# The up projection as seven half products, woven with the gate products of the next pair

## The chip, the cores and the metric

The kernel runs on one core of one Trainium2 chip. The metric is the device time of one execution in microseconds, as the median over runs; three runs of the kernel before gave 1347.74 us in the median (1342.84 to 1347.84). A change of less than 0.5 % (some 7 us) counts as no change here, since that is about what a measurement of this kernel can tell.

Names of engines as in the profile: PE is TensorE (matmul), PEld its weight load, DVE is VectorE, ACT ScalarE, POOL GpSimd, SP the engine that issues the loads.

## The reference, cut to what matters

The program is one inference step of a decoder layer: two token mixers (a Mamba-2 part and an RWKV-7 part), then a SwiGLU feed-forward network, a per-layer embedding gate and a final norm, for 512 prompt tokens and 64 sample tokens (576 columns) at model width 1024. Only the feed-forward network is touched:

```python
hf = rmsnorm(h, w['norm_ffn'])
h = h + (jax.nn.silu(hf @ w['w_gate']) * (hf @ w['w_up'])) @ w['w_down']
```

`w_gate` and `w_up` are 1024 x 2816 (D_FF = 22 tiles of 128 columns), `w_down` is 2816 x 1024, all float32.

## The kernel before, in words

Activations lie transposed: 128 channels on the partitions, 576 tokens in the free dimension, so `hf` is eight tiles of 128x576 (`XF`). Every float32 operand is split into a rounded high part and a low remainder (`split`, L186: ACT copies the high part, DVE or POOL subtracts it for the low part), and each product is three matmuls: high x high, high x low, low x high. A matmul takes 288 of the 576 columns (`HV`).

`linear` (L217) makes one inner tile of 128 channels: two weight blocks of 128x512 are loaded, split (`wsplit`, L196, into `whi`/`wlo`, two buffers each; DVE and POOL take turns with the low part) and used in 24 matmuls each, 48 in all.

The 22 inner tiles are worked off in eleven pairs. Pair 0 is plain: gate and up with `linear`, then `silu`, the product with the up tile, and `inner` (L1350), which splits the result into `ah`/`al` for the down projection; POOL subtracts `al`. From pair 1 on the two gate tiles of a pair are made by `gate_pair` (L1411) after the Strassen-Winograd scheme: the weights of the two tiles are four blocks (upper and lower half of the 1024 channels, first and second tile), the activations four blocks (upper and lower channels, first and second 288 tokens), and seven products of a block with a block, 12 matmuls each, stand for eight, 84 matmuls for 96. For it

- the sums of activation blocks `T1` to `T4` are formed and split once, behind pair 0 (the loop over `k` at L1377 to L1389: per `k` four subtractions on DVE, eight ACT copies and four low parts, two on DVE and two on POOL);
- for each pair the sums of weight blocks `sw` (s1 and s2 and s4 on DVE) and a21 in place (POOL, L1418) are formed;
- each of the seven weight operands is split by `product` (L1398) into `wh`/`wl`, three buffers each;
- five results are kept or joined: ACT copies them out of PSUM (`kept`, tile `e`), POOL adds them (L1429, L1434, L1435), DVE adds from PSUM and multiplies by the norm's `rstd`.

Behind each gate pair its two up tiles come from `linear`. After pair 5 `down(False)` multiplies inner tiles 0 to 11 with `w_down`, after pair 10 `down(True)` the other ten.

Nothing of the order on an engine is as written: the Tile framework schedules the recorded instructions of each engine by its own timeline and hands out the buffers of a tag by it, so an engine's queue is a fixed list, worked off in order, and each instruction waits for its inputs and for its buffer to come free. The weights come from one packed array `wts` in the order of use, by SP.

Of the kernel before, what the change touches and what calls it, by code (L numbers as in the profile page):

```python
# [75 lines left out]
def hybrid_step(ctx, tc, A):  # L76
# [107 lines left out]

    def split(src, pool, tags, shape, lo_eng=None, hi=None, lo=None, hi_eng=None, **kw):
        hi = hi if hi is not None else pool.tile(shape, F32R, tag=tags[0], name=nm(tags[0]), **kw)  # L186
        lo = lo if lo is not None else pool.tile(shape, F32R, tag=tags[1], name=nm(tags[1]), **kw)
# [6 lines left out]
        eng.tensor_tensor(lo[:], src, hi[:].bitcast(F32), ALU.subtract)  # L194
# [1175 lines left out]


# [34 lines left out]
    def kept(ps):  # L1406
        t = cm.tile([P, HALF], F32, tag="e", name=nm("e"), bufs=5)
# [3 lines left out]
    def gate_pair():  # L1411

        a11, a21, a22 = (block() for _ in range(3))
        a12 = block(wp, "raw")
        s1, s2, s4 = (cm.tile([P, 512], F32, tag="sw", name=nm("sw"), bufs=3) for _ in range(3))
# [4 lines left out]
        ab, cc = lin_bank(), lin_bank()  # L1420
        a, b, c = ab[:, 0:HALF], ab[:, 512:512 + HALF], cc[:, 0:HALF]
        sa, sb = ft("sa"), ft("sb")
        product(a, a11, "B11", True, V)
        p1 = kept(a)
        product(b, s2, "T2", True, G)
        p6 = kept(b)
        product(c, s1, "T1", True, V)
        p5 = kept(c)
        G.tensor_tensor(p6[:], p6[:], p1[:], ALU.add)  # L1429
        product(a, a12, "B21", False, G)  # L1430
        V.tensor_tensor(sa[:, N1], a, rs[:, N1], ALU.mult)
        product(b, a21, "T3", False, V)
        p67 = kept(b)
        G.tensor_tensor(p67[:], p67[:], p1[:], ALU.add)  # L1434
        G.tensor_tensor(sb[:, N2], p67[:], p5[:], ALU.add)  # L1435
        product(c, s4, "B22", False, G)
        V.tensor_tensor(sa[:, N2], c, p6[:], ALU.add)
        V.tensor_tensor(sa[:, N2], sa[:, N2], rs[:, N2], ALU.mult)
        product(b, a22, "T4", False, V)
        V.tensor_tensor(sb[:, N1], b, p1[:], ALU.add)  # L1440
        V.tensor_tensor(sb[:], sb[:], rs[:], ALU.mult)
        for s_ in (sa, sb):
            act(s_[:], s_[:], AF.Silu)
        return sa, sb
# [12 lines left out]
    for p in range(1, NFF // 2):  # L1457
        for s_ in gate_pair():
            up = lin_ps()
            linear(XF, up, WLAST)  # L1460
            V.tensor_tensor(s_[:], up, s_[:], ALU.mult)
# [73 lines left out]
def pack(inp):  # L1535
# [79 lines left out]
    for c in range(0, NFF, 2):  # L1615
        if c:
            for ks, i in ((lo4, 0), (lo4, 1), (hi4, 1), (hi4, 0)):
                put(wg, ks, c + i)
        for i in range(2):
            if not c:  # L1620
                put_tile(wg, 0, 8, i)
            put_tile(wu, 0, 8, c + i)
# [50 lines left out]
```

## Time and profile before

| | us |
|---|---|
| median of three runs | 1347.74 |
| span of the profiled execution | 1349.0 |
| PE busy in it | 1246.8 |
| DVE / ACT / POOL busy in it | 826.0 / 618.9 / 625.6 |
| gate and up of pairs 1 to 5 (first product at 885.8, last before the down projection at 1017.5) | 131.7 |
| gate and up of pairs 6 to 10 (1097.0 to 1213.9) | 116.9 |

The span runs from the first to the last instruction; the page names no other time for this execution, and the median run is 1.3 us shorter than its span. The feed-forward network lies between some 875 us and 1287 us. A line of the profile's groups gives source line, engine, operation, output<-inputs, shape and count, then the summed and the mean duration, then the idle time of the engine before these instructions and what ended it.

### The profile page before, as it was taken

What the parts mean: (1) busy time and instruction counts of PE and PEld (TensorE: products, weight loads), DVE (VectorE), ACT (ScalarE), POOL (GpSimd) and SP (SyncE); (2) the same over time, 40 slices, a digit from 0 to 9 for tenths busy, and PEclk for the clock granted to TensorE, in tenths of its full rate; (3) what the DMA queues carried; (4) which work ended last, traced back from release to release, by engine and by line L of the source; (5) the groups of instructions that cost most, each with busy time, mean ns of one, the idle gap of its engine ahead of it and who ended that gap; (6) DMA issues with size and microseconds to landing.
All of it is one profiled execution on the core that took longest, in us unless ns stands there. A gap on an engine that the chain in (4) does not pass through costs nothing.

```text
span 1349.0 us, 26596 instructions
## 1 busy us (share of the span) xinstructions
PE 1246.8 (92%) x10525; PEld 1150.7 (85%) x10525; DVE 826.0 (61%) x1443; ACT 618.9 (46%) x1256; POOL 625.6 (46%) x597
## 2 busy tenths in 40 slices
PE   6897999999989978899999969989999999999997
PEld 6787897889868957788779859889999999999997
DVE  6648666887687785943466667886553135443454
ACT  6565436534654463343434364464442124433363
POOL 5425413642355154122456645565654336654642
PEclk9897799899979978889989989998999999999998
DMA  5322242234232412262454542222323222314322
GB/s 164 125 68 66 77 117 63 85 103 116 75 99 78 109 41 80 94 214 83 157 176 131 179 125 72 73 93 88 92 88 87 79 86 82 93 59 149 96 89 71
DMA packets 94461, 135.58 MB, mean 100 GB/s; under 512 B 34705, under 2 KB 39057, under 8 KB 94337
## 3 DMA queue, kind: packets, MB, share of 16 engines
q1 hardware_dynamic: 93760, 133.36, 32.4%
q8 instruction: 83, 1.36, 0.4%
q10 hardware_dynamic: 576, 0.52, 0.1%
q14 instruction: 42, 0.34, 0.1%
HBM read 106.10 MB, written 27.75 MB: 99 GB/s over the span
## 4 chain that ended last, share of the span: by engine, by line
PE 63%; DVE 14%; ACT 4%; issue 4%; DMA 3%; POOL 3%; DVEq 0%; SPq 0%; ACTq 0%; POOLq 0%
PE lin L234 21%; PE lin L1403 8%; PE lin L223 6%; PE lin L221 6%; PE lin L222 6%; DVE h L395 2%; PE lin L1508 1%; PE lin L1509 1%; PE lin L1510 1%; DVE tmp L674 1%; DVE wlo L206 1%; DVE Tt L676 1%; PE lin L613 1%; PE cx L797 1%; DVE suv L831 1%
## 5 line engine op out<-in xcount | busy, mean ns | idle before, releaser
L206 POOL TENSOR_TENSOR wlo<-raw,whi 128x512 fp32r<-128x512 f32 (+1 forms) x108 | 146.4, 1356 | 352.5 <-ACT whi L93 269.5
L93 ACT ACTIVATE whi<-raw 128x512 fp32r<-128x512 f32 (+1 forms) x232 | 143.3, 618 | 259.1 <-PE lin L234 126.4
L221 PE MATMUL lin<-xhi,whi 128*128 128x288 f32 (+1 forms) x784 | 243.3, 311 | 2.5 <-ACT whi L93 2.2
L223 PE MATMUL lin<-xhi,wlo 128*128 128x288 f32 (+1 forms) x784 | 241.5, 308 | 2.3 <-POOL wlo L206 2.3
L222 PE MATMUL lin<-xlo,whi 128*128 128x288 f32 (+1 forms) x784 | 241.5, 308 | 0.3 <-POOL xlo L194 0.3
L206 DVE TENSOR_TENSOR wlo<-raw,whi 128x512 fp32r<-128x512 f32 (+1 forms) x124 | 100.9, 814 | 103.2 <-PE lin L234 60.4
L221 PEld LDWEIGHTS lin<-xhi,whi 128*128 128x128 f32 (+1 forms) x784 | 151.0, 193 | 9.3 <-ACT whi L93 2.6
L223 PEld LDWEIGHTS lin<-xhi,wlo 128*128 128x128 f32 (+1 forms) x784 | 150.7, 192 | 6.2 <-POOL wlo L206 2.8
L222 PEld LDWEIGHTS lin<-xlo,whi 128*128 128x128 f32 (+1 forms) x784 | 150.8, 192 | 4.8 <-issue 1.2
L234 PE MATMUL lin<-xhi,whi 128*128 128x288 f32 x384 | 62.3, 297 | 3.2 <-ACT xhi L93 3.0
L234 PE MATMUL lin<-xlo,whi 128*128 128x288 f32 x384 | 60.8, 298 | 0.0
L234 PE MATMUL lin<-xhi,wlo 128*128 128x288 f32 x384 | 59.3, 297 | 0.0
L234 PEld LDWEIGHTS lin<-xhi,whi 128*128 128x128 f32 x384 | 54.6, 189 | 3.8 <-ACT xhi L93 1.7
L234 PEld LDWEIGHTS lin<-xlo,whi 128*128 128x128 f32 x384 | 54.8, 191 | 0.0
L234 PE MATMUL lin<-ah,wlo 128*128 128x288 f32 x352 | 54.7, 296 | 0.0
L234 PE MATMUL lin<-al,whi 128*128 128x288 f32 x352 | 54.7, 296 | 0.0
L234 PE MATMUL lin<-ah,whi 128*128 128x288 f32 x352 | 54.7, 296 | 0.0
L234 PEld LDWEIGHTS lin<-xhi,wlo 128*128 128x128 f32 x384 | 54.3, 191 | 0.0
L1403 PE MATMUL lin<-T,wh 128*128 128x288 f32 x320 | 50.1, 296 | 4.5 <-DVE T L194 2.8
L674 DVE TENSOR_TENSOR tmp<-L,Tt 72x30 f32<-72x30 f32 (+14 forms) x120 | 49.2, 410 | 3.2
L234 PEld LDWEIGHTS lin<-ah,whi 128*128 128x128 f32 x352 | 49.6, 189 | 0.0
L234 PEld LDWEIGHTS lin<-ah,wlo 128*128 128x128 f32 x352 | 49.6, 189 | 0.0
(425 smaller groups left out, 3197.8 us busy)
## 6 DMA issues: line engine op xcount, KB each, us to landing
raw<-wts SPq DMA_DIRECT2D x271, 256.0 KB, 2.6
S<-s_wkv SPq DMA_DIRECT2D x8, 512.0 KB, 5.1
hd<-s_ssm SPq DMA_DIRECT2D x8, 512.0 KB, 4.5
o_ssm_s<-hd SPq DMA_DIRECT2D x8, 512.0 KB, 2.9
xbc_d<-E SPq DMA_DIRECT2D x12, 288.0 KB, 2.1
x<-xT SPq DMA_DIRECT2D x8, 288.0 KB
gate_d<-g SPq DMA_DIRECT2D x8, 288.0 KB, 2.5
bv_d<-rw SPq DMA_DIRECT2D x8, 288.0 KB
```

What stands on the lines that cost most here:

```text
L93: return S.activation(out, in_, func, bias=bias, scale=scale)
L206: eng.tensor_tensor(lo[:, 0:n], raw[:, 0:n], hi[:, 0:n].bitcast(F32), ALU.subtract)
L221: T.matmul(ps[:, a:b], whi, xhi[:, a:b], start=first, stop=False)
L222: T.matmul(ps[:, a:b], whi, xlo[:, a:b], start=False, stop=False)
L223: T.matmul(ps[:, a:b], wlo, xhi[:, a:b], start=False, stop=last)
L234: T.matmul(ps[:, a:e], (hi, lo)[p][:, i * P:(i + 1) * P], xs[k + i][q][:, a:e], start=n == k + i == 0, stop=n == 2 and k + i == nk - 1, sk ...
L395: V.scalar_tensor_tensor(h[:], E[:, i:i + 600], w(i), h[:], ALU.mult, ALU.add)
L613: T.matmul(ps[:, c:c + 128].rearrange("p (a t) -> p a t", a=2), s.BK[jj][H[e], g].rearrange("p a t -> p (a t)"), s.G[H[e], g, jj, :, e], s ...
L674: V.tensor_tensor(o, L[:, jx:jx + 1, jx + 1:32].to_broadcast([NB, jx, n]), Tt[:, 0:jx, jx:jx + 1].to_broadcast([NB, jx, n]), ALU.mult)
L676: V.tensor_tensor(Tt[:, 0:jx, jx + 1:32], Tt[:, 0:jx, jx + 1:32], o, ALU.subtract)
L797: T.matmul(uw[H[e], jj, :], TT[H[e], g, jj, :], xs[H[e], jj, :], start=True, stop=True)
L1403: T.matmul(ps, (hi, lo)[p][:, k * P:(k + 1) * P], OPS[n][k][q], start=first and p == q == k == 0, stop=p == 1 and k == 3, skip_group_check ...
```

## The change

Five things, in the words of the diff:

1. The up tiles of a pair are made by seven half products too. `gate_pair` becomes `seven(up, out, order)`, a generator that yields after every product; `weave` runs two of them in turn, the gate of the next pair beside the up of this one. A pair then has 14 products of 12 matmuls in place of 7 and of four times 24.
2. Two pairs are plain instead of one (`for f in range(3)` ahead of the `T` sums and `for f in range(3, 4)` behind them), so nine pairs are left: four in the first weave, five in the second.
3. Joins read PSUM: DVE adds from PSUM to an `e` tile; ACT keeps only the first product, and POOL adds nothing any more. POOL instead forms a21 and s4 of each `seven` and the low part of two of its seven weight operands ("4" and "2"); DVE makes the other five. A fourth PSUM place `d` holds product 4.
4. `inner` no longer has POOL subtract `al` for the first eight of the inner tiles of each down projection: ACT writes minus the source, rounded like the high part, and a DMA issued by POOL adds the source to it (`accum_op`). Tiles 8 and up keep the subtraction.
5. Buffers: seven weight blocks, four `sw`, eight `e`; the reserve for POOL's DMA descriptors is set to 1024 bytes of each partition (no DMA was issued by POOL before). The packed weights are put in the new order.

```diff
+    def below(lo, src, hi, eng):
+        if eng == "D":
+            act(lo, src, scale=-1.0)
+            G.dma_start(lo, src, accum_op=ALU.add)
+        else:
+            eng.tensor_tensor(lo, src, hi.bitcast(F32), ALU.subtract)
...
-        AF2.append(split(s_[:], fp, (f"ah{f}", f"al{f}"), [P, NT], lo_eng=G))
+        AF2.append(split(s_[:], fp, (f"ah{f}", f"al{f}"), [P, NT], lo_eng="D" if f % 12 < 8 else G))
 
-    for f in range(2):
+    for f in range(3):
         ps = lin_ps()
         linear(XF, ps, WLAST)
...
+    for f in range(3, 4):
+        ps = lin_ps()
+        linear(XF, ps, WLAST)
...
-        t = pool.tile([P, 512], F32, tag=tag, name=nm(tag), bufs=3)
+        t = pool.tile([P, 512], F32, tag=tag, name=nm(tag), bufs=7)
...
-    def gate_pair():
-        a11, a21, a22 = (block() for _ in range(3))
-        a12 = block(wp, "raw")
-        s1, s2, s4 = (cm.tile([P, 512], F32, tag="sw", name=nm("sw"), bufs=3) for _ in range(3))
+    def seven(up, out, order):
+        a11, a22, a21, a12 = (block() for _ in range(4))
+        s1, s2, s4 = (cm.tile([P, 512], F32, tag="sw", name=nm("sw"), bufs=4) for _ in range(3))
         V.tensor_tensor(s1[:], a21[:], a22[:], ALU.add)
         V.tensor_tensor(s2[:], s1[:], a11[:], ALU.subtract)
         G.tensor_tensor(a21[:], a11[:], a21[:], ALU.subtract)
-        V.tensor_tensor(s4[:], a12[:], s2[:], ALU.subtract)
...
+        G.tensor_tensor(s4[:], a12[:], s2[:], ALU.subtract)
...
+        def join(dst, ps, x):
+            if up:
+                t = kt()
+                V.tensor_tensor(t[:], ps, x[:], ALU.add)
+                V.tensor_tensor(dst, dst, t[:], ALU.mult)
+            else:
+                V.tensor_tensor(dst, ps, x[:], ALU.add)
+        for step in order:
+            if step == "1":
+                product(a, a11, "B11", True, V)
+                e[1] = kept(a)
+            elif step == "6":
+                product(b, s2, "T2", True, V)
+                e[2] = kt()
+                V.tensor_tensor(e[2][:], b, e[1][:], ALU.add)
+            elif step == "4":
+                product(d, a22, "T4", True, G)
+            elif step == "7":
+                product(b, a21, "T3", False, V)
+                e[3] = kt()
+                V.tensor_tensor(e[3][:], b, e[1][:], ALU.add)
+                join(sb[:, N1], d, e[3])
+            elif step == "5":
+                product(c, s1, "T1", True, V)
+                join(sb[:, N2], c, e[3])
+                if not up:
+                    V.tensor_tensor(sb[:], sb[:], rs[:], ALU.mult)
+                    act(sb[:], sb[:], AF.Silu)
+            elif step == "2":
+                product(a, a12, "B21", False, G)
+                V.tensor_tensor(sa[:, N1], a, (sa if up else rs)[:, N1], ALU.mult)
+            else:
+                product(c, s4, "B22", False, V)
+                join(sa[:, N2], c, e[2])
+                if not up:
+                    V.tensor_tensor(sa[:, N2], sa[:, N2], rs[:, N2], ALU.mult)
+                    act(sa[:], sa[:], AF.Silu)
+            yield
+    def weave(pairs, first):
+        queue = [(up, out) for out in ([] for _ in range(pairs)) for up in (False, True)]
+        live, n = [], 0
+        while live or queue:
+            if queue and (not live or len(live) == 1 and n >= (1 if first else 4)):
+                up, out = queue.pop(0)
+                live.append((seven(up, out, "1647523" if first else "1647523"), up, out))
+                n = 0
+                first = first and not up
+            for t in list(live):
+                if next(t[0], 1):
+                    live.remove(t)
+                    if t[1]:
+                        for s_ in t[2]:
+                            inner(s_)
+            n += 1
...
-    for p in range(1, NFF // 2):
-        for s_ in gate_pair():
-            up = lin_ps()
-            linear(XF, up, WLAST)
-            V.tensor_tensor(s_[:], up, s_[:], ALU.mult)
-            inner(s_)
-        if p == NSPLIT - 1:
-            down(False)
+    weave(NSPLIT - 2, True)
+    down(False)
+    weave(NFF // 2 - NSPLIT, False)
...
-    nc = _bacc.Bacc("TRN2", target_bir_lowering=False, num_devices=1)
+    nc = _bacc.Bacc("TRN2", target_bir_lowering=False, num_devices=1, dynamic_dma_scratch_size=1024)
```

Ahead of the feed-forward network no engine's queue differs. Inside it three places carry the prediction.

DVE in the middle of the first weave before (a row is source line, operation, output<-inputs, shape; L1416, L1417, L1419 are s1, s2, s4 of the next gate, L194 and L206 low parts of weights, L1440 and L1461 reads of PSUM, L1441 a product in SBUF):

```order
L1416 TENSOR_TENSOR sw_10994<-raw_1733_10988,raw_1734_10990 128x512
L1461 TENSOR_TENSOR sa_10722<-lin_10854,sa_10722 128x576
L1417 TENSOR_TENSOR sw_10995<-sw_10994,raw_1732_10986 128x512
L1419 TENSOR_TENSOR sw_10996<-raw_10992,sw_10995 128x512
L1440 TENSOR_TENSOR sb_10723<-lin_10720,e_10740 128x288
L194 TENSOR_TENSOR wl_11042<-sw_10994,wh_11041 128x512
L1441 TENSOR_TENSOR sb_10723<-sb_10723,rstd_9895 128x576
L206 TENSOR_TENSOR wlo_11169<-raw_11166,whi_11168 128x512
```

DVE in the change, in the second half of a pair of the first weave (L1436 and L1437 are s1 and s2 of the gate after the next, L191 low parts, L1454, L1479 and L1463 reads of PSUM, L1475 a product in SBUF; `sb` and `sa` are the gate tiles, `lin_11131` belongs to the up):

```order
L1436 TENSOR_TENSOR sw_11269<-raw_1801_11265,raw_1800_11263 128x512
L1454 TENSOR_TENSOR sb_10979<-lin_10977,e_11094 128x288
L191 TENSOR_TENSOR wl_11187<-sw_10971,wh_11186 128x512
L1479 TENSOR_TENSOR sa_10978<-lin_10976,rstd_9895 128x288
L1475 TENSOR_TENSOR sb_10979<-sb_10979,rstd_9895 128x576
L1437 TENSOR_TENSOR sw_11270<-sw_11269,raw_1799_11261 128x512
L1463 TENSOR_TENSOR e_11184<-lin_11131,e_11149 128x288
L191 TENSOR_TENSOR wl_11222<-raw_1773_11120,wh_11221 128x512
L1454 TENSOR_TENSOR sa_10978<-lin_10977,e_11031 128x288
L191 TENSOR_TENSOR wl_11243<-sw_11124,wh_11242 128x512
L191 TENSOR_TENSOR wl_11281<-raw_1799_11261,wh_11280 128x512
```

The same stretch holds more low parts and more short joins, and s4 has left the queue.

POOL beside it, in the change (L1439 is s4, L1438 a21, L191 low parts, L189 the issue of an adding transfer):

```order
L1439 TENSOR_TENSOR sw_11126<-raw_1774_11122,sw_11125 128x512
L191 TENSOR_TENSOR wl_11152<-raw_1741_10967,wh_11151 128x512
L189 DMA al_1763_11069<-sa_10724 128x576
L1438 TENSOR_TENSOR raw_1801_11265<-raw_1799_11261,raw_1801_11265 128x512
L191 TENSOR_TENSOR wl_11206<-raw_1772_11118,wh_11205 128x512
L1439 TENSOR_TENSOR sw_11271<-raw_1802_11267,sw_11270 128x512
L191 TENSOR_TENSOR wl_11299<-raw_1774_11122,wh_11298 128x512
```

POOL's queue now alternates between a sum that needs DVE's s1 or s2 and the low part that PE needs, with the transfers between; the adds of `e` tiles are gone.

PE before, while the `T` sums are being made (L1403 is a product, L234 a plain matmul of `linear`; a row with x2 is both halves of the columns):

```order
L1403 MATMUL lin_10159<-T_1571_10067,wh_10198 128x288
L234 MATMUL lin_10292<-xhi_9634,whi_10325 128x288 x2
L234 MATMUL lin_10292<-xhi_9675,whi_10325 128x288 x2
L234 MATMUL lin_10292<-xhi_9716,whi_10325 128x288 x2
L234 MATMUL lin_10292<-xhi_9757,whi_10325 128x288 x2
L234 MATMUL lin_10292<-xlo_9635,whi_10325 128x288 x2
L234 MATMUL lin_10292<-xlo_9676,whi_10325 128x288 x2
L1403 MATMUL lin_10158<-T_1573_10069,wh_10180 128x288
```

PE in the change at the end of the second plain pair (L241 a plain matmul, L1424 a product; `lin_10422` is the first gate, `lin_10477` its up):

```order
L241 MATMUL lin_10340<-xhi_9634,wlo_10374 128x288 x2
L241 MATMUL lin_10340<-xhi_9675,wlo_10374 128x288 x2
L241 MATMUL lin_10340<-xhi_9716,wlo_10374 128x288 x2
L241 MATMUL lin_10340<-xhi_9757,wlo_10374 128x288 x2
L1424 MATMUL lin_10422<-xlo_9553,wh_10426 128x288
L1424 MATMUL lin_10422<-xlo_9594,wh_10426 128x288
L1424 MATMUL lin_10422<-xhi_9471,wl_10427 128x288
L1424 MATMUL lin_10422<-xhi_9511,wl_10427 128x288
```

Before, products with `T` stand between the plain matmuls as soon as one part of `T` is expected; in the change all 96 plain matmuls of inner tile 3 and the first product of the gate stand ahead of any matmul with `T`, and the up's first product follows.

More of the change, by code (lines that the diff above doesn't have):

```diff
@@ L192, in split @@
         flip[0] += 1
-        eng = lo_eng or (G if flip[0] % 2 else V)
-        eng.tensor_tensor(lo[:], src, hi[:].bitcast(F32), ALU.subtract)
+        below(lo[:], src, hi[:], lo_eng or (G if flip[0] % 2 else V))
         return hi, lo
@@ L1390, in hybrid_step @@
         OPS[n] = [tuple(XF[k0 + k][i][:, c] for i in range(2)) for k in range(4)]
+    for f in range(3, 4):
+        ps = lin_ps()
+        linear(XF, ps, WLAST)
+        if f == 0:
+            up = lin_ps()
+            linear(XF, up, WLAST)
+            rs = rstd_of(st)
+        s_ = ft("sg")
+        V.tensor_tensor(s_[:], ps, rs[:], ALU.mult)
+        act(s_[:], s_[:], AF.Silu)
+        if f:
+            up = lin_ps()
+            linear(XF, up, WLAST)
+        V.tensor_tensor(s_[:], up, s_[:], ALU.mult)
+        inner(s_)
     def block(pool=cm, tag="raw2"):
-        t = pool.tile([P, 512], F32, tag=tag, name=nm(tag), bufs=3)
+        t = pool.tile([P, 512], F32, tag=tag, name=nm(tag), bufs=7)
         nc.sync.dma_start(t[:], A["wts"][wat[0]:wat[0] + P * 512].rearrange("(p n) -> p n", p=P))
@@ L1406, in kept @@
     def kept(ps):
[L1407 removed]
+        t = cm.tile([P, HALF], F32, tag="e", name=nm("e"), bufs=8)
         act(t[:], ps)
         return t
[L1411 to L1415 removed]
+    def seven(up, out, order):
+        a11, a22, a21, a12 = (block() for _ in range(4))
+        s1, s2, s4 = (cm.tile([P, 512], F32, tag="sw", name=nm("sw"), bufs=4) for _ in range(3))
         V.tensor_tensor(s1[:], a21[:], a22[:], ALU.add)
@@ L1418, in gate_pair @@
         G.tensor_tensor(a21[:], a11[:], a21[:], ALU.subtract)
-        V.tensor_tensor(s4[:], a12[:], s2[:], ALU.subtract)
[L1420 to L1444, printed above, removed]
+        G.tensor_tensor(s4[:], a12[:], s2[:], ALU.subtract)
+        ab, cd = lin_bank(), lin_bank()
+        a, b, c, d = (t[:, i:i + HALF] for t in (ab, cd) for i in (0, 512))
+        kt = lambda: cm.tile([P, HALF], F32, tag="e", name=nm("e"), bufs=8)
+        if not up:
+            out += [ft("sa"), ft("sb")]
+        sa, sb = out
+        e = [None] * 4
@@ new lines, in join @@
+        def join(dst, ps, x):
[32 more added lines that the diff above has]
+                join(sa[:, N2], c, e[2])
+                if not up:
+                    V.tensor_tensor(sa[:, N2], sa[:, N2], rs[:, N2], ALU.mult)
+                    act(sa[:], sa[:], AF.Silu)
+            yield
@@ L1616, in pack @@
         if c:
[L1617 to L1622, printed above, removed]
+            for w in (wg, wu) if c >= 4 else ():
+                for ks, i in ((lo4, 0), (hi4, 1), (lo4, 1), (hi4, 0)):
+                    put(w, ks, c + i)
+        for i in range(4) if not c else ():
+            put_tile(wg, 0, 8, i)
+            put_tile(wu, 0, 8, i)
         if c // 2 in (NSPLIT - 1, NFF // 2 - 1):
```

1 line of the change is left out of this document (added).

## The prediction

> **What bounds the kernel now.** I read the page's busy times first, then the busy times by stretch, then what PE waits for, then the single instructions of one pair.
>
> ```profile
> span 1349.0 us, 26596 instructions
> PE 1246.8 (92%) x10525; PEld 1150.7 (85%) x10525; DVE 826.0 (61%) x1443; ACT 618.9 (46%) x1256; POOL 625.6 (46%) x597
> ...
> core 0: us, PE busy (x) PEld busy (x) DVE busy (x) ACT busy (x) POOL busy (x), PEclk, DMA share, GB/s
> 860.00:870.00 10.00, 7.60 (x59) 7.14 (x58) 9.57 (x7) 3.97 (x7) 7.69 (x5) 1.00 0.17 54
> 900.00:910.00 10.00, 6.74 (x47) 5.98 (x45) 9.79 (x14) 6.37 (x14) 7.46 (x8) 1.00 0.08 26
> 910.00:920.00 10.00, 8.75 (x45) 8.76 (x46) 3.41 (x6) 2.72 (x5) 2.90 (x3) 0.66 0.29 82
> 920.00:930.00 10.00, 9.76 (x74) 9.56 (x73) 8.38 (x11) 4.35 (x9) 6.24 (x5) 1.00 0.24 78
> 955.30:979.30 24.00, 24.00 (x184) 24.00 (x183) 12.69 (x16) 11.14 (x21) 14.06 (x11) 1.00 0.32 95
> ```
>
> In a settled pair (955.3 to 979.3) PE is busy without a gap and the other engines about half the time. PE alone bounds it. The exception is the start, 900 to 930, where DVE is full and PE is not. What PE waits for from 876 to 1290 is all there:
>
> ```profile
> PE lin L1403 <- DVE T L194: 2.8, 1, 2.8
> PE lin L1403 <- ACT T L93: 1.7, 2, 1.0
> ...
> 963.27 1.60 PE lin L1403 x12
> 964.87 3.18 PE lin L234 x24
> ```
>
> The last two rows are from the chain of waits and give the price of a matmul: 3.18 us / 24 = 0.1325 us.
>
> **What the change removes on PE.** Four plain tiles more, two less: before, 2 plain tiles x 2 x 48 + 10 x (84 + 96) = 1992 matmuls; after, 4 x 2 x 48 + 9 x 168 = 1896. Minus 96 matmuls x 0.1325 = **-12.7 us**. All of it lies on the path as long as PE stays full. A pair falls from 180 x 0.1325 = 23.9 to 168 x 0.1325 = 22.3 us.
>
> **The start.** From 900 to 930 PE did 47 + 45 + 74 = 166 matmuls where 3 x 75.5 = 226 fit. The 60 missing cost 60 x 0.1325 = 8.0 us: the waits for `T` (4.5 us), then a stretch at a granted clock of 0.66. Forming `T` keeps DVE from
>
> ```profile
> 889.12 1.69 DVE L1382 TENSOR_TENSOR tt<-xa 128x288 f32<-128x288 f32 x1
> ...
> 911.12 0.44 DVE L194 TENSOR_TENSOR T<-xb,T 128x288 fp32r<-128x288 f32 x1
> ```
>
> that is 22.4 us. In the change PE meanwhile has the up of tile 2 (48), tile 3 (96) and the first products of gate and up (24): 168 x 0.1325 = 22.3 us. The work just covers; I keep 1.5 us for the first matmuls with `T`, and take **-6.5 us** (bounds -4 to -8).
>
> **What the change adds on the other engines.** The rows of 926 to 1020 (pairs 2 to 5 of the kernel before), by form:
>
> ```profile
> L194 DVE TENSOR_TENSOR wl<-raw,wh 128x512 fp32r<-128x512 f32 x12 | 10.9, 912 | 5.5 <-ACT wh L93 5.5
> L1417 DVE TENSOR_TENSOR sw<-sw,raw 128x512 f32<-128x512 f32 x4 | 5.3, 1335 | 0.0
> L1416 DVE TENSOR_TENSOR sw<-raw,raw 128x512 f32<-128x512 f32 x4 | 3.1, 784 | 2.2 <-DMA raw<-wts 2.1
> L1441 DVE TENSOR_TENSOR sb<-sb,rstd 128x576 f32<-128x576 f32 x5 | 7.0, 1406 | 2.1 <-POOL sb L1435 2.1
> L1431 DVE TENSOR_TENSOR sa<-lin,rstd 128x288 f32<-128x288 f32 x4 | 1.8, 458 | 17.1 <-PE lin L1403 17.1
> L1438 DVE TENSOR_TENSOR sa<-sa,rstd 128x288 f32<-128x288 f32 x4 | 1.8, 451 | 0.0
> ...
> L1418 POOL TENSOR_TENSOR raw<-raw,raw 128x512 f32<-128x512 f32 x5 | 7.0, 1396 | 13.7 <-DVE sw L1416 13.7
> L194 POOL TENSOR_TENSOR al<-sa,ah 128x576 fp32r<-128x576 f32 x5 | 9.0, 1805 | 0.0
> L194 POOL TENSOR_TENSOR wl<-raw,wh 128x512 fp32r<-128x512 f32 x4 | 5.6, 1408 | 2.2 <-ACT wh L93 2.2
> ...
> L93 ACT ACTIVATE wh<-raw 128x512 fp32r<-128x512 f32 x16 | 10.0, 625 | 10.0 <-PE lin L1403 4.7 <-POOL wlo L206 3.1 <-issue 2.2
> L93 ACT ACTIVATE e<-lin 128x288 f32<-128x288 f32 x15 | 5.6, 401 | 3.9 <-PE lin L1403 3.9
> L93 ACT ACTIVATE ah<-sa 128x576 fp32r<-128x576 f32 x5 | 3.4, 683 | 0.9 <-DVE sa L1461 0.8
> ```
>
> A pair then asks of DVE 10 low parts x 0.91, two s1 x 0.78, two s2 x 1.34, twelve joins from PSUM x 0.46, four short SBUF products x 0.45 and one `sb` x `rstd` of 1.41: 9.1 + 1.6 + 2.7 + 5.5 + 1.8 + 1.4 = 22.1 us, against 12.7 before. Of ACT 14 x 0.63 + 2 x 0.40 + 6 x 0.68 = 13.7 us, in most pairs with two more copies for `al`: 15.1. Of POOL 4 x 1.41 + 4 x 1.40 = 11.2 us and two transfers to issue. ACT and POOL fit into 22.3; **DVE is as long as PE.** What a pair costs is decided there.
>
> ```profile
> 882.29 0.69 DVE L206 TENSOR_TENSOR wlo<-raw,whi 128x512 fp32r<-128x512 f32 x1 [1.93 <-PE lin L234]
> 882.90 0.69 DVE L1416 TENSOR_TENSOR sw<-raw,raw 128x512 f32<-128x512 f32 x1
> 883.50 0.75 DVE L1363 TENSOR_TENSOR sg<-lin,rstd 128x576 f32<-128x576 f32 x1
> ...
> 991.48 1.88 POOL L194 TENSOR_TENSOR al<-sa,ah 128x576 fp32r<-128x576 f32 x1
> 993.32 1.25 POOL L1435 TENSOR_TENSOR sb<-e,e 128x288 f32<-128x288 f32 x1
> ...
> 992.07 1.83 DVE L206 TENSOR_TENSOR wlo<-raw,whi 128x512 fp32r<-128x512 f32 x1
> 993.83 0.44 DVE L1440 TENSOR_TENSOR sb<-lin,e 128x288 f32<-128x288 f32 x1
> ```
>
> The DVE means hold a stall. With POOL idle a 128x512 subtract starts 0.61 us after the last one; with POOL on `al` the same subtract took 1.83 us and ended 0.54 us after POOL's end (993.36). A read of PSUM took 0.44 us though POOL ran. So the two engines take turns when both operands lie in SBUF: a meeting costs DVE what is left of POOL's instruction.
>
> [...]
>
> I walk the second half of a pair with that (the DVE and POOL rows shown with the change). From the end of product 5 PE has 4 + 12 + 8 + 12 + 4 matmuls before product 7, and 8 more before it needs that low part: 48 x 0.1325 = 6.4 us. DVE and POOL take turns meanwhile: s1 0.6, a21 1.4, low part 0.6, POOL's low part 1.4, `sb` x `rstd` 0.7, s2 0.6, s4 1.4, low part of product 7 0.6: 7.3 us, the reads of PSUM hidden beside POOL. PE waits 0.9 us there. The next low part but one (product 1 of the next gate) meets POOL's low part of product 2, for 0 or 1.2 us, as it falls. The first half has room: seen the same way its low parts end 0.6 us or more before their use. So PE waits 0.9 to 2.1 us a pair; the last pair of each weave has no s1 and s2 of a following one, and so less. I take **1.0 us for each of nine pairs, +9 us**.
>
> Bounds of this term: 0 (the queues meet less often than walked), and 2.7 a pair: 2.1 and another 0.6 where the issue of a transfer holds POOL longer than the 1.0 us that I allow. The trace has no DMA issued by POOL; the nearest row is the subtract it replaces, 1.8 us, which is nearly the upper end, and nothing is the lower. The landing of the transfer has no reader before the down projection. ACT's second copy (0.68) stands ahead of the high part of the second product behind it, with 1.6 us of room.
>
> **Sum.** 1349.0 - 12.7 - 6.5 + 9.0 = 1338.8 us of span. The median of the runs lies 1.3 us below that span: **1338 us** (1337.5), 0.7 % faster.
>
> **Rivals.**
>
> *All waits are hidden* (0 to 0.4 a pair): 1347.7 - 19.2 + 2 = 1330 us. For it: PE had no wait in any settled pair; against it: DVE was then half idle. 0.13.
>
> *The gain is given back* (1.4 to 2.8 us a pair, about 2.1): 1347.7 - 19.2 + 19 = 1347 us. This is the change not doing what it says: PE has less to do and waits as much longer. For it: the second meeting of the walk, lost each time. 0.25.
>
> *The shared turn becomes the bound*, and the kernel slower. Per pair the SBUF instructions of both engines, one after the other, are 14 x 0.61 + 0.7 + 4 x 0.4 + 8 x 1.4 = 22.0 us; the reads of PSUM (twelve, at 0.4 us from start to start) add 4.8 where they don't fall beside POOL. If none does, a pair takes 26.8 us, PE waits 4.5, and the time is 1347.7 - 19.2 + 40 = 1369 us; with half of them, 24.4 and 1347. It is slower than before by over 0.5 % from 2.9 us a pair, when under a third falls beside POOL. In pairs whose `al` stays on POOL (three of nine) 2 x 1.5 us are added. For it: DVE's sum of 22.1; against it: 993.83, where a read did fall beside POOL. I give 0.16, and say 1358.
>
> *The clock falls.* After the waits for `T` the granted clock was 0.66 from 910 to 920 (45 matmuls in 8.75 us), though in 860 to 870, with PE busy 7.60 of 10, it stayed at 1.00. Some 3 us were lost by it. If it came in every pair: 1338 + 27 = 1365 us. The waits of my walk are about 1 us among 22 of work, less than in 860 to 870. 0.03.
>
> [...]
>
> **How the numbers follow.** My forecast (0.4 to 1.4 us a pair, 1332 to 1341 us) has 0.43, and with the hidden case 0.56 lies below 1341, faster by over 0.5 % (about what a measurement can tell from no change). The range runs from 1327 (-8.0 at the start, no waits) to 1355 (-4 and 2.7 us a pair: 1347.7 - 16.7 + 24.3); it leaves out most of the last two rivals. Within 0.5 %: 0.25; slower: 0.19.
>
> **What would show it.** PE's matmuls fall by 96. Right: a settled pair of 23 to 23.7 us with PE's waits on DVE low parts, ahead of product 7 and of the next product 1; DVE busy above 85 % in the weaves; no stretch near 900 at a lower clock. Wrong: PE without waits (1330), or waits for POOL's low parts, for ACT, or for weights (`raw2`), which I price at nothing because seven buffers let a load run ahead by most of a pair. The prediction fails most easily on the 1.0 us: each 0.8 us a pair more is 7 us.

## The result, and the profile after

| | us (median) | against the kernel before on the same chip |
|---|---|---|
| the kernel before | 1345.29 (1339.39 to 1347.84) | |
| the changed kernel | 1330.51 (1329.64 to 1330.91) | 0.989, 95 % interval 0.9861 to 0.9919 |
| the changed kernel on a second chip | 1336.34 (1332.71 to 1342.39), before 1343.09 | 0.9956, 0.9935 to 0.9977 |

The change makes the kernel faster, by 1.1 % in the first comparison and 0.4 % in the second. The second is less than the 0.5 % that counts as a change here, though its interval lies below 1. The two intervals do not overlap, and the first experiments below show where such a difference can come from. The forecast was 1338 us, 0.7 % faster.

The page of the changed kernel (engine, busy time, share, instructions):

```profile
span 1328.8 us, 26626 instructions
PE 1225.6 (92%) x10429; PEld 1127.1 (85%) x10429; DVE 887.1 (67%) x1570; ACT 631.1 (47%) x1274; POOL 611.6 (46%) x583
```

PE has its 96 matmuls less (10525 to 10429) and DVE 61 us more. The busy times by stretch, in the columns of the prediction (stretch, its length, PE, PEld, DVE, ACT, POOL, granted clock, DMA):

```profile
900.00:910.00 10.00, 10.00 (x77) 10.00 (x77) 9.82 (x15) 6.62 (x15) 6.21 (x7) 1.00 0.35 82
910.00:920.00 10.00, 10.00 (x77) 10.00 (x77) 5.42 (x9) 5.91 (x12) 6.85 (x6) 1.00 0.58 163
920.00:930.00 10.00, 9.72 (x73) 9.52 (x73) 9.94 (x14) 3.05 (x5) 6.62 (x5) 1.00 0.29 80
930.00:940.00 10.00, 7.04 (x47) 6.57 (x46) 8.54 (x13) 6.46 (x13) 3.77 (x4) 0.94 0.37 91
940.00:950.00 10.00, 10.00 (x70) 9.99 (x70) 6.35 (x11) 3.80 (x7) 6.28 (x5) 0.89 0.40 102
1124.70:1147.60 22.90, 22.66 (x170) 22.29 (x169) 20.53 (x33) 12.45 (x22) 13.98 (x11) 1.00 0.46 119
```

The start, where PE stood still before, is full: DVE works at the `T` sums (900 to 910, 9.82 of 10) while PE has 77 matmuls. There is a new hole at 930 to 940 (47 matmuls), where the first gate and the first up end. A settled pair is the last row: 22.9 us, DVE busy for 20.5 of them, no hole to be seen. What PE waits for from 870 to 1290 (us in total, times, longest):

```profile
PE lin L1424 <- ACT e L93: 2.2, 1, 2.2
PE lin L1424 <- DVE e L1469: 1.5, 5, 0.4
PE lin L1424 <- DVE wl L191: 0.8, 1, 0.8
PE lin L1424 <- ACT wh L93: 0.4, 2, 0.2
```

The waits for low parts (`wl` of DVE) that the prediction put into every pair are one wait of 0.8 us in all.

**Three parts of the time.** To compare executions I split each at the first matmul of the feed-forward norm (the split: 868.6 us in the kernel before, 859.5 in the changed one; ahead of it both have the same queues, with the first 46 matmuls of the network at their end). "Rest" runs from there to the end. "Network" runs from the first feed-forward matmul behind that norm to the start of the last one of the down projection: 3002 matmuls before, 2906 in the change. "Lost" is the network less the time that its matmuls take back to back, 1.0667 / 8 = 0.1333 us each, as the plain ones of the first down projection show in the changed kernel (start, length, instruction):

```profile
1043.27 1.23 PE L241 MATMUL lin<-ah,whi 128*128 128x288 f32 x8
1044.34 1.23 PE L241 MATMUL lin<-al,whi 128*128 128x288 f32 x8
```

| execution | split | rest | network | lost |
|---|---|---|---|---|
| before, profiled first | 868.6 | 480.5 | 409.4 | 9.4 |
| before, with the reserve for descriptors alone | 869.9 | 474.6 | 404.3 | 4.2 |
| before, again | 865.0 | 477.1 | 406.8 | 6.8 |
| before, second plain pair alone | 867.2 | 473.7 | 402.8 | 1.2 |
| changed, profiled first | 859.5 | 469.2 | 398.1 | 10.9 |
| changed, again | 867.7 | 467.1 | 397.2 | 10.0 |
| changed, one plain pair | 863.3 | 480.7 | 409.2 | 25.2 |
| changed, without POOL's low parts | 867.9 | 466.2 | 395.2 | 8.0 |
| changed, s4 on DVE | 865.6 | 470.2 | 399.2 | 12.0 |
| changed, first up after four products | 858.9 | 469.1 | 397.7 | 10.5 |
| changed, no adding transfers | 864.5 | 477.9 | 407.0 | 19.8 |
| changed, each up after five products | 863.9 | 495.4 | 425.3 | 38.1 |
| changed, low part of 4 by transfer | 862.3 | 470.9 | 400.7 | 13.5 |
| changed, four buffers for the parts | 862.6 | 470.4 | 400.3 | 13.1 |

Of the 20.2 us between the first two spans (1349.0 and 1328.8), 9.0 lie ahead of the split, where nothing was changed, and 11.3 in the network.

Each row is one execution. The three rows of the kernel before without a second plain pair lie up to 5.9 us apart in the rest, the two of the changed kernel 2.1 us, so a difference of a few us between two rows is not yet an effect of the edit. Nor does the price of 0.1333 us hold everywhere. In the second down projection of the changed kernel the same plain matmuls follow one another faster:

```profile
1244.28 1.20 PE L241 MATMUL lin<-ah,whi 128*128 128x288 f32 x8
1245.32 1.20 PE L241 MATMUL lin<-al,whi 128*128 128x288 f32 x8
```

Eight take 1.04 us there, 0.130 each; the kernel before has 0.1333 in both down projections. Over the 480 matmuls this is 1.2 us of the 11.3, in both profiles of the changed kernel. It is no wait, the prediction has no term for it, and its cause is open. Of the runs built on the change, three do not have it (first up after four, each up after five, four buffers); their "lost" is some 1.2 us larger for this reason.

### The profile page after: what moved, and what is told of

Its sections match the earlier page's. It is cut to its first block, busy times and chain, and to the rows that moved or that the text cites. A ratio compares the mean times of both kernels' runs of the same rounds, so it can differ in the third digit from the quotient of the medians.

```text
span 1328.8 us, 26626 instructions
## 1 busy us (share of the span) xinstructions
PE 1225.6 (92%) x10429; PEld 1127.1 (85%) x10429; DVE 887.1 (67%) x1570; ACT 631.1 (47%) x1274; POOL 611.6 (46%) x583
## 5 line engine op out<-in xcount | busy, mean ns | idle before, releaser
L213 POOL TENSOR_TENSOR wlo<-raw,whi 128x512 fp32r<-128x512 f32 (+1 forms) x92 | 125.4, 1363 | 307.9 <-ACT whi L93 230.3
L93 ACT ACTIVATE whi<-raw 128x512 fp32r<-128x512 f32 (+1 forms) x200 | 123.2, 616 | 213.3 <-PE lin L241 94.9
L213 DVE TENSOR_TENSOR wlo<-raw,whi 128x512 fp32r<-128x512 f32 (+1 forms) x108 | 83.5, 774 | 73.5 <-PE lin L241 37.7
L1424 PE MATMUL lin<-T,wh 128*128 128x288 f32 x576 | 87.3, 296 | 2.6 <-ACT e L93 2.2
L1424 PEld LDWEIGHTS lin<-T,wh 128*128 128x128 f32 x576 | 80.2, 190 | 3.3 <-ACT e L93 2.4
L93 ACT ACTIVATE wh<-raw 128x512 fp32r<-128x512 f32 x72 | 45.1, 629 | 53.9 <-PE lin L1424 37.1
L191 POOL TENSOR_TENSOR wl<-raw,wh 128x512 fp32r<-128x512 f32 x36 | 57.1, 1586 | 13.1 <-PE lin L1424 7.5
L191 DVE TENSOR_TENSOR wl<-sw,wh 128x512 fp32r<-128x512 f32 x54 | 50.8, 940 | 8.6 <-ACT wh L93 4.5
L241 PE MATMUL lin<-ah,whi 128*128 128x288 f32 x352 | 54.7, 294 | 0.0
L241 PE MATMUL lin<-al,whi 128*128 128x288 f32 x352 | 54.4, 295 | 0.0
L241 PE MATMUL lin<-ah,wlo 128*128 128x288 f32 x352 | 54.2, 295 | 0.0
L1424 PE MATMUL lin<-T,wl 128*128 128x288 f32 x288 | 50.2, 299 | 0.0
L241 PEld LDWEIGHTS lin<-ah,whi 128*128 128x128 f32 x352 | 49.3, 188 | 0.0
L241 PEld LDWEIGHTS lin<-al,whi 128*128 128x128 f32 x352 | 49.2, 188 | 0.0
L241 PEld LDWEIGHTS lin<-ah,wlo 128*128 128x128 f32 x352 | 49.2, 188 | 0.0
```

Of the source, the lines that this page charges most:

```text
L93: return S.activation(out, in_, func, bias=bias, scale=scale)
L191: eng.tensor_tensor(lo, src, hi.bitcast(F32), ALU.subtract)
L213: eng.tensor_tensor(lo[:, 0:n], raw[:, 0:n], hi[:, 0:n].bitcast(F32), ALU.subtract)
L241: T.matmul(ps[:, a:e], (hi, lo)[p][:, i * P:(i + 1) * P], xs[k + i][q][:, a:e], start=n == k + i == 0, stop=n == 2 and k + i == nk - 1, sk ...
L1424: T.matmul(ps, (hi, lo)[p][:, k * P:(k + 1) * P], OPS[n][k][q], start=first and p == q == k == 0, stop=p == 1 and k == 3, skip_group_check ...
```

## The experiments

The medians and ratios of each group are against the kernel before on the chip of that group. With every edit the framework draws up all queues of the network anew, so a run differs in the order of instructions too, not only in the edited work. The chips of these groups are on record, that of the first comparison is not. On the third and fourth chip the changed kernel itself was not run; its two ratios above are 0.989 and 0.9956, so ratios between them do not rank a variant against it.

**The same two kernels again, and the reserve alone** (second chip, the kernel before 1343.09 us). The reserve alone:

```diff
-    nc = _bacc.Bacc("TRN2", target_bir_lowering=False, num_devices=1)
+    nc = _bacc.Bacc("TRN2", target_bir_lowering=False, num_devices=1, dynamic_dma_scratch_size=1024)
```

> The kernel before, with only the 1024 bytes reserved for POOL's DMA descriptors. The two traces split at the first matmul of the feed-forward norm: 868.6 us before and 859.5 after, and from there to the end 480.5 and 469.3. Theory 1 (the 9.0 us ahead of the split are the granted clock of that one execution, not the change): from the split to the end 480.5 within 1 us, the split anywhere from 859 to 870, and a median within 0.5 % of the kernel before. Theory 2 (the reserve shifts something ahead of the feed-forward network): the split at 859 to 861 and a median of 1336 to 1340 us.

> The changed kernel once more, unaltered, for a second profile. Theory 1 (the split varies by execution): from the split to the end 469.3 within 1 us, the split anywhere from 859 to 870. Theory 2 (the change shortens what lies ahead of the split): the split again at 859 to 860.

The reserve alone gave 1340.39 us, ratio 0.999 (0.9965 to 1.0014), split at 869.9: no effect that the measurement shows. The changed kernel gave 1336.34, and its split lay at 867.7, 8.2 us later than in its first profile. Busy times from the start to the split, of the kernel before, then of the changed kernel's first and second profile:

```profile
0.00:868.60 868.60, 782.06 (x6986) 689.36 (x6986) 593.08 (x1129) 421.85 (x901) 377.37 (x407) 0.92 0.35 107
```
```profile
0.00:859.50 859.50, 772.89 (x6984) 680.69 (x6984) 593.30 (x1129) 421.05 (x901) 377.29 (x407) 0.93 0.35 108
```
```profile
0.00:867.70 867.70, 784.00 (x6984) 690.86 (x6984) 593.52 (x1129) 422.75 (x901) 377.65 (x407) 0.92 0.35 107
```

DVE, ACT and POOL have the same instructions and the same busy time within 2 us; only PE's busy time moves, 772.9 against 782.1 and 784.0, for the same matmuls, and the granted clock with it (0.93 against 0.92 and 0.92). So most of the 9.0 us belong to one execution, not to the change: 8.2 of them were absent when the same kernel ran again. PE's busy time alone does not set the split, though: the run with the reserve has the latest one, 869.9, with PE busy for 777.8 us. Over all fourteen profiles the split lies at 865.0 to 869.9 in the four built on the kernel before and at 858.9 to 867.9 in the ten built on the change. The ranges overlap, but their means differ by some 4 us; the chips differ too, and whether a part of that is the change's stays open.

The expectation for the rest of the reserve's run (480.5) was wrong, at 474.6. The kernel before once more (fifth group, 1346.13 us against 1343.85, 1.0018, 0.9995 to 1.004), unaltered:

> The kernel before once more, unaltered, for a third look at its start (the second was that with the reserve alone). Lost at the start by products waiting for T: 8.2 us in the first profile, where the clock was halved for 6.8 us right behind the waits, 3.0 in the second, where it was not. Theory 1 (the waits alone cost 3 to 5 us, and the halved clock comes with some executions): 3 to 5 us lost without a halved clock there, or 7 to 9 with one; from the first product with T the waits come from DVE's sums in either. Theory 2 (the reserve made the difference): 8 us again with the clock at half. The split lies from 859 to 870 us, from there to the end 474 to 481.

What PE waits for at the start, in the run with the reserve and in the kernel before again:

```profile
PE lin L1403 <- DVE T L194: 1.0, 1, 1.0
PE lin L1403 <- ACT T L93: 0.9, 2, 0.6
```
```profile
PE lin L1403 <- DVE T L194: 2.8, 1, 2.8
PE lin L1403 <- ACT T L93: 1.8, 2, 1.1
```

and the busy times of the kernel before again, at the start:

```profile
897.00:907.00 10.00, 6.33 (x44) 5.58 (x42) 9.79 (x14) 5.97 (x14) 7.45 (x8) 1.00 0.08 26
907.00:917.00 10.00, 9.13 (x69) 9.14 (x70) 5.04 (x9) 3.72 (x8) 2.55 (x3) 1.00 0.42 133
```

The waits of 4.6 us are those of the first profile (4.5), but the clock stayed at 1.00 behind them where it was 0.66 in the first from 910 to 920 (0.50 from 911 to 917). Behind the first product 5.5 us are lost without the halved clock and 8.3 with it; with the reserve the same waits came to 1.9 (3.0 us lost). Why these were shorter there was not pursued; the instructions are the same. What decides whether the clock falls behind such waits no run here shows.

**One plain pair more or less** (same chip). The second plain pair alone in the kernel before, and the change without it:

```diff
-    for f in range(2):
+    for f in range(3):
...
+    for f in range(3, 4):
...
-    for p in range(1, NFF // 2):
+    for p in range(2, NFF // 2):
```

> The kernel before with a second plain pair behind the T sums and nine in place of ten of its own pairs; nothing else of the change. 12 matmuls more, +1.6 us. Theory 1 (the plain pair covers the T sums): the 8.4 us lost at the start go, so from the split to the end 480.5 + 1.6 - 8.4 = 473.7 us, and a median 6 to 7 us under the kernel before. Theory 2 (the sums are only late elsewhere): 480 to 482 us and no gain.

```diff
-    for f in range(3):
+    for f in range(2):
...
-    for f in range(3, 4):
+    for f in range(2, 2):
...
-    weave(NSPLIT - 2, True)
+    weave(NSPLIT - 1, True)
```

> The changed kernel without its second plain pair (ten woven pairs in place of nine): 24 matmuls fewer, -3.2 us. Theory 1 (the plain pair covered the T sums): some 8 us of waits and low clock come back, from the split to the end 469.3 - 3.2 + 8.4 = 474.5 us, 5 us over the changed kernel; more if the up's products, which need T as well, wait too (up to 478). Theory 2 (the cover was not needed): 466 us.

The plain pair alone gave 1337.69 us, 0.9957 (0.9936 to 0.9979), rest 473.7 as expected. Its lost time falls to 1.2 us: PE no longer waits for `T`. The change without it gave 1346.11, 1.0027 (1.0007 to 1.0047), rest 480.7, 2.7 us beyond the upper end of what was expected. What PE waits for at its start, and the busy times there:

```profile
PE lin L1424 <- ACT T L93: 9.8, 4, 4.6
```
```profile
897.00:907.00 10.00, 4.35 (x14) 3.32 (x15) 7.36 (x13) 4.28 (x11) 4.44 (x5) 0.50 0.21 48
```

Gate and up side by side come to `T` sooner, wait 9.8 us for it, and the clock is at 0.50 through the whole of this stretch. Theory 1 holds: without the second plain pair the seven products for the up gain nothing (0.3 % slower, within the 0.5 % that counts as no change). With it, on one chip, the medians are 1337.69 for the plain pair alone and 1336.34 for the whole change, a difference that these medians cannot tell from nothing. In the network it is 402.8 to 397.2: 108 matmuls fewer, 108 x 0.1333 = 14.4 us, of which 8.8 come back as lost time.

**Taking POOL's work out of DVE's way** (third chip, the kernel before 1344.84 us).

```diff
+        if eng is G:
+            hi = cm.tile([P, 512], F32R, tag="wh", name=nm("wh"), bufs=3)
+            act(hi[:], w[:])
+            lo = hi
+        else:
+            hi, lo = split(w[:], cm, ("wh", "wl"), [P, 512], lo_eng=eng, bufs=3)
```

> The changed kernel with the low parts of products 4 and 2 left out (their high part is used in its place, so the output lacks these terms); PE's matmuls are the same, POOL loses four subtractions a pair, some 6.4 us. A settled pair of the changed kernel lasts 22.95 us, 0.55 of it waits, with DVE busy 20.3. Theory 1 (DVE and POOL take turns, so DVE's busy time holds POOL's): DVE's busy time in a pair falls by 1.5 us or more though it has the same instructions, PE's waits in a pair fall under 0.2 us, from the split to the end 467.1 - 3 = 464 us, and less if the 4.5 us at the first change of pairs go too (460). Theory 2 (DVE's queue is simply long): DVE stays at 20.3 us, 467 us.

1334.35 us, 0.9917 (0.9892 to 0.9943). A settled pair:

```profile
1132.40:1155.60 23.20, 22.98 (x171) 22.44 (x169) 19.68 (x32) 12.70 (x23) 6.75 (x7) 1.00 0.45 118
```

POOL's busy time is halved (13.98 to 6.75), DVE's falls by 0.85 us, and the pair is no shorter (23.2 and 23.4 against 22.9). The 5.5 us at the first change of pairs went to 0.8. In the weaves PE now waits for something else:

```profile
PE lin L1429 <- ACT wh L93: 1.7, 9, 0.2
```

The five waits for L1469, a read of PSUM by DVE (1.5 us), are gone; these nine for ACT's high parts, and one of 0.8 us for another read, stand in their place. So neither theory holds as a whole. DVE's time did fall, but by less than 1.5 us; without POOL's subtractions the hole and the waits for L1469 go, and a pair is still no shorter. Whether the new waits come from the edit itself (a high part that also serves as the low one is needed for longer) or from the new order was not tested.

```diff
-        G.tensor_tensor(s4[:], a12[:], s2[:], ALU.subtract)
+        V.tensor_tensor(s4[:], a12[:], s2[:], ALU.subtract)
```

> The changed kernel with s4 on DVE in place of POOL. Theory 1 (taking turns): DVE's own work grows by 2 x 0.68 us a pair, but the 1.5 us products held by s4 on POOL fall to 0.45, so DVE stays at 20 to 21 us and PE's waits at 0.55 or less: from the split to the end 464 to 467.5 us. Theory 2 (the sum of DVE's work counts): DVE 21.7 us a pair, waits up by 0.5 to 1 us a pair, 472 to 476 us.

1335.57 us, 0.9924 (0.9897 to 0.995), rest 470.2, between what the two theories gave. Groups of DVE from 1100 to 1192 (count, busy, mean ns), in the changed kernel and with s4 on DVE:

```profile
L191 DVE TENSOR_TENSOR wl<-sw,wh 128x512 fp32r<-128x512 f32 x24 | 20.6, 858 | 4.0 <-PE lin L1424 3.0 <-ACT wh L93 1.0
L191 DVE TENSOR_TENSOR wl<-raw,wh 128x512 fp32r<-128x512 f32 x16 | 10.9, 678 | 0.0
L1484 DVE TENSOR_TENSOR sa<-sa,rstd 128x288 f32<-128x288 f32 x5 | 7.3, 1468 | 0.0
...
L1437 DVE TENSOR_TENSOR sw<-sw,raw 128x512 f32<-128x512 f32 x7 | 5.7, 819 | 0.0
```
```profile
L1437 DVE TENSOR_TENSOR sw<-sw,raw 128x512 f32<-128x512 f32 x8 | 11.7, 1457 | 0.0
```

and one pair with s4 on DVE:

```profile
1133.00:1157.20 24.20, 22.81 (x170) 22.37 (x169) 21.29 (x34) 12.55 (x23) 10.43 (x9) 1.00 0.45 113
```

The stall moves: in the changed kernel the short product of L1484 (0.45 us in the kernel before) takes 1.47 us, since s4 on POOL runs beside it; with s4 on DVE it is s2 (L1437) that takes 1.46 instead of 0.82, beside POOL's next low part. DVE's pair grows to 21.3, the pair to 24.2 (the pairs beside it take 23.3 and 24.1). Theory 1's 20 to 21 us for DVE were too low.

```diff
-        AF2.append(split(s_[:], fp, (f"ah{f}", f"al{f}"), [P, NT], lo_eng="D" if f % 12 < 8 else G))
+        AF2.append(split(s_[:], fp, (f"ah{f}", f"al{f}"), [P, NT], lo_eng=G))
```

> The changed kernel without the adding transfers: POOL subtracts all al again, 14 of them in the weaves, 1.8 us each in place of a transfer's 0.88 us; ACT loses 16 copies. Theory 1 (taking turns): the subtractions hold DVE by up to 1.8 us each, PE's waits grow by 0.5 to 1.5 us a pair, from the split to the end 470 to 477 us. Theory 2 (POOL is idle 41 % of a pair, so its work is free): 467 us.

1340.60 us, 0.9972 (0.9949 to 0.9996), rest 477.9:

```profile
1136.20:1160.10 23.90, 22.98 (x170) 22.40 (x169) 22.18 (x32) 11.54 (x20) 15.53 (x12) 1.00 0.31 90
```

A pair costs 0.9 us more with DVE at 22.2 us for the same instructions, though POOL is idle for a third of it. Theory 1 holds, with a rest 0.9 us above its range; the adding transfers are worth about 9 us of network (407.0 against 397.2 and 398.1).

**Where the up begins** (third and fourth chip; the kernel before 1344.84 and 1343.44 us).

```diff
-            if queue and (not live or len(live) == 1 and n >= (1 if first else 4)):
+            if queue and (not live or len(live) == 1 and n >= 4):
```

> The changed kernel with the first up begun after four gate products in place of one, as in all other pairs. Theory 1 (the 4.5 us lost some 30 us behind the first product come from the first gate and up ending together, with their joins and the next pair's first sums on DVE at once): they go, 1 to 2 us of waits for T come, from the split to the end 464 us. Theory 2 (the loss is the price of the first full change of pairs, wherever it falls): 467 us.

1332.83 us, 0.9909 (0.9882 to 0.9935). The hole at the first change of pairs is gone (1.3 us in place of 5.5 in the same stretch), so theory 1 is right about the place; but the rest is 469.1, not 464. Where a part of it went, in order of time:

```profile
883.77 1.01 POOL L189 DMA_DIRECT2D al<-sg  x1
...
884.50 1.57 POOL L213 TENSOR_TENSOR wlo<-raw,whi 128x512 fp32r<-128x512 f32 x1
...
886.13 1.32 PE L241 MATMUL lin<-xhi,wlo 128*128 128x288 f32 x8 [1.22 <-POOL wlo L213]
```

Another schedule of the plain pair put the issue of a transfer ahead of a low part on POOL, and PE waits 1.22 us there. Another 1.3 us lie in the second down projection, whose matmuls follow one another after 0.133 us here and after 0.131 in the changed kernel; small waits make up the remainder.

```diff
-            if queue and (not live or len(live) == 1 and n >= (1 if first else 4)):
+            if queue and (not live or len(live) == 1 and n >= 5):
```

> The changed kernel with each up, and each next gate, begun after five products of the other in place of four (the first up after five in place of one). Theory 1 (the waits come from where joins, low parts and POOL's sums happen to meet, so another offset gives other waits of like size): a settled pair 22.7 to 23.4 us, the 4.5 us at the first change of pairs gone as with four, from the split to the end 466 to 472 us. Theory 2 (four was the offset at which the queues just fit): 1 us a pair more, 477 us.

1357.10 us, 1.0086 (1.0058 to 1.0114), rest 495.4: both theories were far too low. A pair:

```profile
1125.10:1153.10 28.00, 25.03 (x170) 23.94 (x169) 20.86 (x32) 12.68 (x22) 13.03 (x11) 0.94 0.39 97
```

and what happens at its end, in order of time:

```profile
1151.83 1.42 POOL L191 TENSOR_TENSOR wl<-raw,wh 128x512 fp32r<-128x512 f32 x1
1151.91 2.88 DVE L1452 TENSOR_TENSOR sa<-sa,e 128x288 f32<-128x288 f32 x1
...
1153.11 1.36 POOL L1439 TENSOR_TENSOR sw<-raw,sw 128x512 f32<-128x512 f32 x1
1154.72 0.44 DVE L1469 TENSOR_TENSOR e<-lin,e 128x288 f32<-128x288 f32 x1
...
1155.31 0.77 PE L1424 MATMUL lin<-xhi,wh 128*128 128x288 f32 x4 [1.93 <-DVE e L1469]
```

A product of 0.45 us lasts 2.88, through two of POOL's instructions and to 0.3 us behind the second; the read of PSUM behind it is late, and PE waits 1.93 us for it. Such a wait stands in four pairs of the second weave; in the first weave the same read costs 0.6 to 0.7 us twice. It is not the whole loss: of 20.6 us of waits in the weaves 9.1 are for L1469, 6.2 for L1463, another read of PSUM, and 5.3 for ACT's high parts. The pair takes 28.0 us though DVE has no more to do, and the granted clock is 0.94 in the mean, 0.06 x 28.0 / 0.5 = 3.4 us at half, right behind the long wait (0.50 from 1156 to 1159). Three of the four long waits have such a stretch behind them, the fourth does not. So five is much worse than four, and the length of a pair hangs on where the queues meet; no other offset was run.

**Two attempts at the waits that are left** (fourth chip), both with the first up after four products:

```diff
-                product(d, a22, "T4", True, G)
+                product(d, a22, "T4", True, "D")
```

> The first up after four products, and the low part of product 4 by an adding transfer (ACT writes minus the weights, a DMA issued by POOL adds them) in place of POOL's subtraction. POOL gives up 2 x 1.61 us of SBUF work a pair and issues two transfers of 0.88 us more. Theory 1 (taking turns): DVE's busy time in a pair falls by 0.6 to 1.2 us, waits by 0.2 to 0.5, from the split to the end 465 to 468 us. Theory 2 (the sum lands too late): PE waits 1 to 2 us in each of 18 products 4, 485 to 505 us.

```diff
-        hi, lo = split(w[:], cm, ("wh", "wl"), [P, 512], lo_eng=eng, bufs=3)
+        hi, lo = split(w[:], cm, ("wh", "wl"), [P, 512], lo_eng=eng, bufs=4)
...
-        t = cm.tile([P, HALF], F32, tag="e", name=nm("e"), bufs=8)
+        t = cm.tile([P, HALF], F32, tag="e", name=nm("e"), bufs=6)
```

> The first up after four products, four buffers each for the high and low parts of weights in place of three, and to make room six e tiles in place of eight. Theory 1 (ACT and DVE make the parts late because a buffer comes free late: ACT's high parts wait for PE in most cases): parts are made up to 1.6 us earlier, a settled pair goes from 22.95 to 22.5 us, from the split to the end 464 to 466 us. Theory 2 (the waits come from DVE's reads of PSUM held up by POOL, which more buffers do not touch): 469 us, or up to 475 where six e tiles are too few.

1334.44 us (0.9918, 0.9888 to 0.9949) and 1334.93 (0.9925, 0.99 to 0.995). The pair with the low part by transfer:

```profile
1141.30:1164.20 22.90, 22.84 (x171) 22.37 (x169) 19.29 (x32) 14.08 (x24) 12.31 (x11) 1.00 0.61 141
```

The transfer lands in time but for two waits of 1.1 us in all, DVE is relieved by 1.2 us as theory 1 had it, and the pair still takes 22.9 us: PE waits for DVE's low parts and ACT's high parts instead of L1469. Its rest of 470.9 lies outside both theories. Four buffers leave it at 22.9 to 23.1 with seven waits for L1469: its theory 2. The rest of 470.9 and 470.4 is no gain over the changed kernel. No run beat it by more than the measurement tells.

## Why the prediction was right, and where its steps were off

**The time.** The forecast, 1338 us or 0.7 % faster, lies between the two measurements (1.1 % and 0.4 %). For the feed-forward network it said -10.2 us; the first profiles give -11.3, the second one of the changed kernel -9.6 or -7.1 (406.8 and 404.3 to 397.2). The 1330.5 measured first is the number of the rival "All waits are hidden", but not for its reason: 10 us are lost in the weaves. The term that was off is the first one of "1349.0 - 12.7 - 6.5 + 9.0 = 1338.8 us of span". It takes the 868 us ahead of the network as fixed; they were 9.0 us shorter in the first execution of the changed kernel and 0.9 in the second.

**PE's matmuls, -12.7 us.** Right: 3002 to 2906, 96 x 0.1333 = 12.8. That one price holds for every matmul was not: the second down projection gave 1.2 us more.

**The start, -6.5 us (-4 to -8).** The mechanism was right: `T` waits of 4.5 us before, none after, the last sum on DVE ends at 910.2 us and the first matmul with `T` starts at 912.1; both plain-pair runs show it. The size was that of one execution: the start of the kernel before lost 8.3 us in its first profile, 3 of them by the clock, 5.5 in the next and 3.0 with the reserve, so that two of the three lie outside the range of 4 to 8. The 1.5 us kept for the first matmuls with `T` were not needed.

**The waits, +9.0 us.** The sum was right, by luck: 10.0 us lost in the weaves in the first profile and 9.0 in the second. Its parts were not. "1.0 us for each of nine pairs" is 0.5 to 0.6 (22.9 to 23.0 us a pair against 168 x 0.1333 = 22.4), and 4.3 to 5.5 us lie in one place, the first change of pairs. In order of time, changed kernel:

```profile
931.89 1.29 POOL L1438 TENSOR_TENSOR raw<-raw,raw 128x512 f32<-128x512 f32 x1 [3.06 <-DVE sw L1436]
932.04 1.69 DVE L191 TENSOR_TENSOR wl<-raw,wh 128x512 fp32r<-128x512 f32 x1
...
933.66 2.21 DVE L191 TENSOR_TENSOR wl<-sw,wh 128x512 fp32r<-128x512 f32 x1
933.74 1.57 POOL L191 TENSOR_TENSOR wl<-raw,wh 128x512 fp32r<-128x512 f32 x1
...
935.79 0.45 DVE L1484 TENSOR_TENSOR sa<-sa,rstd 128x288 f32<-128x288 f32 x1
...
936.27 0.68 ACT L93 ACTIVATE sa<-sa 128x576 f32<-128x576 f32 x1 [3.24 <-DVE sa L1484]
...
937.38 0.39 ACT L93 ACTIVATE e<-lin 128x288 f32<-128x288 f32 x1
937.82 1.58 PE L1424 MATMUL lin<-T,wh 128*128 128x288 f32 x8 [2.18 <-ACT e L93]
```

Two low parts of DVE are held by POOL (1.69 and 2.21 us in place of 0.68); L1484 behind them is late; ACT's `Silu` waits for that; and the copy of product 1 out of PSUM, which PE needs, stands behind `Silu` and one high part in ACT's queue. The step had walked DVE and POOL but not this third queue. The walk's places (low parts ahead of product 7 and of the next product 1) came up once, 0.8 us. In the settled pairs the waits are for L1469, a read of PSUM behind a held product:

```profile
1145.67 1.67 POOL L1439 TENSOR_TENSOR sw<-raw,sw 128x512 f32<-128x512 f32 x1 [3.23 <-DVE wl L191]
...
1146.12 1.53 DVE L1484 TENSOR_TENSOR sa<-sa,rstd 128x288 f32<-128x288 f32 x1
...
1147.22 0.69 PE L1424 MATMUL lin<-xhi,wl 128*128 128x288 f32 x4
...
1147.58 0.44 DVE L1469 TENSOR_TENSOR e<-lin,e 128x288 f32<-128x288 f32 x1
...
1148.17 0.77 PE L1424 MATMUL lin<-xhi,wh 128*128 128x288 f32 x4 [0.25 <-DVE e L1469]
```

In the changed kernel this is most of the 0.5 us: four matmuls that take 0.53 us back to back begin 0.95 us ahead of the next, so the wait costs 0.4 us there, more than the 0.25 of recorded idle time. But the meeting is not what keeps the pair at its length. With half of POOL's work gone, or DVE relieved by 1.2 us, the waits for L1469 went, others for ACT's high parts and DVE's low parts came, and the pair stayed at 22.9 to 23.4. Why no variant came below 22.9 stays open.

**Its own signs.** DVE was busy for 90 % of a settled pair, above the 85 % named, and the pair of 22.9 us lies just under 23 to 23.7. But a wait for ACT, which the prediction named as a sign of being wrong and for which its sum had no term, was the longest of all, 2.2 us.

**Taking turns.** Right for single instructions: the rows above have short SBUF products of DVE that end some 0.3 us behind POOL's instruction (1.53 us for L1484, 2.88 for L1452, in place of 0.45). DVE's 20.5 us a pair are under the 22.1 of the sum: its low parts took (20.6 + 10.9) / 40 = 0.79 us where 0.91 was assumed, and the stalls that are left fell on L1484 and its like.

**The rivals on the slower side.** The shared turn did not become the bound. The run with an offset of five has a pair as long, 28.0 us (26.3 without the 1.7 lost to the halved clock) beside the 26.8 worked out for no overlap at all, but not by that mechanism: DVE was busy for 20.9 us of it, and the time went into late reads and waits for ACT. Against the rival of the clock in each pair (0.03) stood that the walked waits are about 1 us among 22 of work. In that run one wait of 1.93 us, 3.8 us behind one of 0.48, had a stretch at a granted clock of 0.50 to 0.55 behind it in three cases of four.

## What to carry to other kernels

Before a difference is explained by the change, split the two traces where the programs begin to differ, and compare the unchanged part: here it moved by 9 us, as much as the change is worth. Take more than one profile of each kernel: its lost time alone lay between 4.2 and 9.4 us in three executions of the kernel before. When a wait is walked through two queues, follow it through every queue that stands between the late instruction and the engine that counts. And try the plain part of a change by itself: one more plain pair, without any of the new products, gave 5.4 of the 6.8 us in the medians of the chip where both ran. (In the network the traces divide it otherwise: from 404.3 to 409.4 us down to 402.8 by the plain pair, and 5.6 more by the rest of the change.)
